# One decoder trunk on one core: adaLN dot products with a loading step of their own, spread over the GLU and the first MLP, and group 6 of that MLP as block products

## The chip, the cores and the metric

The kernel runs on one core of one Trainium2 chip. The metric is the device time of one execution in microseconds (us), the median over several runs; lower is better.

## The reference

The program computes a trunk of two layers on x of 1024 tokens by 1024 features, in float32. Each sub-layer is preceded by an RMS norm that is scaled and shifted by values which depend on one vector c ("adaLN"), and its result is gated by a third such value. Cut to what matters here:

```python
def ada_chunks(c, w, b, n):
    m = jnp.einsum('bd,de->be', jax.nn.silu(c), w) + b
    return jnp.split(m, n, axis=-1)
...
    for i in range(DEPTH):                       # DEPTH = 2
        sh_a, sc_a, g_a, sh_m, sc_m, g_m = ada_chunks(c, ada_w[i], ada_b[i], 6)
        if i < N_A_LAYERS:                       # layer 0: S5 and a GLU
            h = modulate(rms_norm(x, mix_norm_g[i]), sh_a, sc_a)
            y = s5_mixer(h, ...)
            val, gate = jnp.split(jnp.einsum('bsd,de->bse', jax.nn.gelu(y), s5_w_glu[j]), 2, axis=-1)
            mix = val * jax.nn.sigmoid(gate)
        else:                                    # layer 1: attention
            kv_shift, kv_scale = ada_chunks(c, kv_ada_w, kv_ada_b, 2)
            hkv = modulate(rms_norm(x, kv_norm_g), kv_shift, kv_scale)
            ...
        x = x + g_a[:, None, :] * mix
        h = modulate(rms_norm(x, mlp_norm_g[i]), sh_m, sc_m)
        ff = jnp.einsum('bsf,fd->bsd', jnp.square(jax.nn.relu(jnp.einsum('bsd,df->bsf', h, mlp_w1[i]))), mlp_w2[i])
        x = x + g_m[:, None, :] * ff
```

The 112 columns of 128 values that all `ada_chunks` yield together are 112 matrix rows of dot products with silu(c).

## The kernel before

**Stages.** The work runs through S5 (0 to about 235 us of the profile), the GLU (to 411), the first MLP (to about 1130), attention (to about 1850) and the second MLP. Features lie on partitions, tokens in the free dimension in two halves h of 512.

**Matrix products.** TensorE works on fp32r values, so each float32 operand is split into a high and a low part and each product is three matmuls of 128x512 (`mm3`, L251 to L253). A weight unit of 128x1024 is loaded by SyncE's queue into a tile `raw`, cast by ScalarE to its high part `uh` (L217), and VectorE subtracts to get `ul` (`split_unit`, L84). The pool of `raw` tiles has three buffers.

**Dot products.** A dot product (`gemv`, L177) loads 128x1024 of the adaLN weights into a tile of the same pool, and VectorE multiplies it by the row `silr` and sums it into one column of `mod` (or `bias`, for 24 that come from `wT`). After eight of them a small addition ends the chunk, and some chunks also give a column block of `scl`.

**Keep jobs.** GpSimd (POOL) prepares attention's weights meanwhile: `keep` loads 128x512 (L231), scales it (L78; not for `wo`), casts the high part (L236), subtracts (L84) and writes both parts to device memory (`kh`, `kl`, L239). There are 16 jobs for `wo`, 32 for `wkv`, 16 for `wq`; the last 48 need `scl` columns of the chunk M_KSC. Two pairs of tiles `e` take turns.

**GLU.** For output block i of 8 and half h, `glu(i, h)` makes 48 matmuls, ScalarE's sigmoid `g`, VectorE's `g` times the value product, and the gated sum into `xall`. Then follows the norm of the MLP: for each half a small chain on `rw` gives the reciprocal root, and `norm.apply` makes for each k of 8 a tile f (L93, `f<-xall,scl,f`), its high part on ScalarE and its low part `h` (L93, `h<-f,mod,h`), which the next matmuls read. Half 0 is applied around glu(7, 1), half 1 in the first part of the MLP.

**First MLP.** The hidden dimension is cut into 8 groups c of four blocks. Group 0's four up products run for half 0, then for half 1 (the "first part"); after that each group's down products run between the up products of the next group. An up product's result goes through ReLU on ScalarE (`ra`, `rb`), is squared on VectorE and split into `f` tiles. In the second MLP, groups 1 to 7 use `seven`: the 2x2 block products of the down step as seven instead of eight, with POOL making the combined weight blocks.

**Order.** The program is written as engine calls, and a scheduler that works with its own estimates sets each engine's order when the program is built. Calls `pump(n)` in the source take the next jobs (dot products and keep jobs mixed) off a queue and emit them there: nine after each GLU block, three or four at each `mid`, which stand between the steps of the MLP groups.

Of the kernel before, what the change touches and what calls it, by code (L numbers as in the profile page):

```python
# [13 lines left out]
ALU = mybir.AluOpType  # L14
# [42 lines left out]
def kernel(ctx, tc, A, out):  # L57
# [47 lines left out]
    def open_x(i):  # L105
        es = ExitStack()
        pools["x"] = es.enter_context(tile_pool(f"xp{i}", bufs=16 if i else 1))
        pools["raw"] = es.enter_context(tile_pool(f"raw{i}", bufs=3))
        es.callback(pools.pop, "raw")
        turns.clear()  # L110
        return es

    def open_ax(i):
        es = ExitStack()
        pools["ax"] = es.enter_context(tile_pool(f"pax{i}", bufs=4 if "pv" in pools else 6, space=PSUM))
        return es
# [16 lines left out]
    def open_pv():  # L133
        es = ExitStack()
        pools["pv"] = es.enter_context(tile_pool("ppv", bufs=2, space=PSUM))
# [88 lines left out]
    def keep(key, src, c, scale=None):  # L224
# [653 lines left out]
    class Inner:  # L878
# [37 lines left out]
    def mlp(layer, xs, hs, norm, fs, mid=None, done=None, place=None):  # L916
# [124 lines left out]
        def fast(c):  # L1041
            return layer == 1 and c > 0
# [443 lines left out]
    pools["un"] = ctx.enter_context(tile_pool("unp", bufs=3))  # L1486
# [4 lines left out]
    rowp = ada_es.enter_context(tile_pool("rowp", bufs=1))  # L1491
# [295 lines left out]
```

## Time and profile before

| | |
|---|---|
| median of 3 runs | 2519.7 us (2517.2 to 2522.97) |
| profiled execution | 2516.43 us, span 2514.7 us |
| mean granted TensorE clock | 0.974 of 2.4 GHz |
| TensorE busy | 93% of the span |
| VectorE busy | 70% |
| ScalarE busy | 37% |
| GpSimd busy | 36% |

The span goes from the first to the last instruction; the execution's own time is 1.7 us longer. Busy shares are means over stages with different limits.

### The profile page before, as it was taken

The page shows a single profiled execution, that of the slowest core. Times are in us where ns is not written, and L with a number is a line of the kernel's source. Part 1 is how long each engine was busy: PE and PEld are TensorE (multiplying, and loading weights), DVE is VectorE, ACT ScalarE, POOL GpSimd, SP SyncE. Part 2 cuts the span into 40 slices and gives each one's busy share as a digit, 9 for nine tenths or more (in the row PEclk, how much of TensorE's full clock was granted, in tenths as well). Part 3 has the DMA queues.
Part 4 walks back from the last instruction along what each step waited for, and adds up shares of the span by engine and source line. Part 5 has one row for each costly group of instructions (what it writes and reads, how often), then busy time and mean ns, then how long its engine had stood idle before and what let it go on. Part 6 is the DMA issues. An engine that isn't in the chain of part 4 may idle for free.

```text
span 2514.7 us, 33271 instructions
## 1 busy us (share of the span) xinstructions
PE 2350.6 (93%) x12552; PEld 1979.3 (79%) x12552; DVE 1754.3 (70%) x2570; ACT 941.8 (37%) x1710; POOL 909.5 (36%) x965
## 2 busy tenths in 40 slices
PE   3888999989999999999899999998999999999998
PEld 2677788867778888888888888887778888888886
DVE  7997557766776545345687877788583667876787
ACT  5653124211111222133566666676351232223221
POOL 4664460378775000014333323343110322342334
PEclk8899999999999999998999999999999999999999
DMA  4225863667766333123211111126721011111112
GB/s 150 86 79 188 283 221 105 216 241 251 252 239 217 101 117 126 45 89 102 81 58 39 64 68 68 59 100 213 250 78 57 34 51 59 60 42 51 56 54 76
DMA packets 105344, 297.08 MB, mean 118 GB/s; under 512 B 13280, under 2 KB 25568, under 8 KB 105184
## 3 DMA queue, kind: packets, MB, share of 16 engines
q1 hardware_dynamic: 87264, 240.42, 27.9%
q0 software_dynamic: 15360, 50.34, 5.5%
q10 hardware_dynamic: 2560, 4.20, 0.7%
q8 instruction: 99, 1.62, 0.3%
q14 instruction: 61, 0.50, 0.1%
HBM read 241.23 MB, written 49.48 MB: 116 GB/s over the span
## 4 chain that ended last, share of the span: by engine, by line
PE 61%; DVE 17%; DMA 11%; issue 5%; ACT 2%; POOL 1%; SPq 0%; DVEq 0%; POOLq 0%; ACTq 0%
DMA raw<-in_adaT_dram 8%; PE pm L70 8%; PE pm L251 8%; PE pm L252 8%; PE pm L253 8%; PE pa L1001 3%; PE pa L999 3%; PE pa L1000 3%; PE pt L70 3%; DVE sn L1282 3%; DVE raw L177 2%; PE pa L253 2%; PE pa L251 2%; PE pa L252 2%; PE po L70 2%
## 5 line engine op out<-in xcount | busy, mean ns | idle before, releaser
L251 PE MATMUL pm<-h,uh 128*128 128x512 f32 x1192 | 465.6, 393 | 19.3 <-ACT rb L927 15.8
L253 PE MATMUL pm<-h,ul 128*128 128x512 f32 x1192 | 465.5, 391 | 4.7 <-DVE ul L84 4.7
L252 PE MATMUL pm<-h,uh 128*128 128x512 f32 x1192 | 466.3, 391 | 1.6 <-DVE h L93 1.6
L217 ACT CAST uh<-raw 128x1024 fp32r<-128x1024 f32 x130 | 136.7, 1051 | 486.9 <-PE pa L252 154.5
L84 DVE TENSOR_TENSOR ul<-raw,uh 128x1024 fp32r<-128x1024 f32 (+1 forms) x158 | 202.7, 1283 | 126.5 <-ACT uh L217 103.8
L251 PEld LDWEIGHTS pm<-h,uh 128*128 128x128 f32 x1192 | 225.0, 189 | 71.5 <-ACT rb L927 19.3
L177 DVE CUSTOM_DVE_ANT_0 raw<-raw,silr 128x1024 f32<-128x1024 f32 x119 | 162.5, 1369 | 155.4 <-DMA raw<-in_adaT_dram 140.6
L253 PEld LDWEIGHTS pm<-h,ul 128*128 128x128 f32 x1192 | 225.1, 189 | 52.5 <-DVE ul L84 5.6
L252 PEld LDWEIGHTS pm<-h,uh 128*128 128x128 f32 x1192 | 225.3, 189 | 48.6 <-DVE h L93 2.2
L70 PE MATMUL pm<-uh,h 128*128 128x256 f32 x1024 | 238.5, 301 | 3.8 <-DVE rs L1138 3.0
L1282 DVE TENSOR_TENSOR_SCAN sn<-sn 128x768 f32<-128x768 f32 (+7 forms) x128 | 180.6, 1417 | 46.5 <-ACT sn L1277 45.2
L81 POOL TENSOR_TENSOR f<-f,f 128x512 f32<-128x512 f32 x30 | 44.0, 1468 | 397.3 <-ACT f L831 397.2
L70 PEld LDWEIGHTS pm<-uh,h 128*128 128x128 f32 x1024 | 181.7, 199 | 5.0 <-DVE rs L1138 3.4
L81 POOL TENSOR_TENSOR raw<-raw 128x256 f32<-128x256 f32 x28 | 26.0, 929 | 411.4 <-DVE ul L84 411.4
L251 PE MATMUL pa<-f,uh 128*128 128x512 f32 x396 | 154.4, 390 | 1.7 <-DVE xall L93 1.0
L252 PE MATMUL pa<-f,uh 128*128 128x512 f32 x396 | 154.1, 389 | 0.0
L253 PE MATMUL pa<-f,ul 128*128 128x512 f32 x396 | 153.7, 389 | 0.0
L70 PE MATMUL pm<-ul,h 128*128 128x256 f32 x512 | 148.7, 290 | 0.9 <-DMA ul<-kl 0.9
L78 POOL TENSOR_TENSOR sg<-sg,sn 128x512 f32<-128x512 f32 x64 | 93.0, 1453 | 122.5 <-DVE sn L1282 56.3
L70 PE MATMUL pm<-h,uh 128*128 128x512 f32 x402 | 133.7, 414 | 0.0
L93 DVE SCALAR_TENSOR_TENSOR x<-pa,mod,x 128x512 f32<-128x512 f32 x143 | 103.3, 743 | 43.5 <-PE pa L253 29.6
L1277 ACT ACTIVATE sn<-z,rrr 128x512 f32<-128x512 f32 (+1 forms) x192 | 111.6, 581 | 46.9 <-PE z L70 45.4
(380 smaller groups left out, 5497.7 us busy)
## 6 DMA issues: line engine op xcount, KB each, us to landing
raw<-in_w_dram SPq DMA_DIRECT2D x140, 512.0 KB, 3.3
raw<-in_adaT_dram SPq DMA_DIRECT2D x96, 512.0 KB, 3.7
uh<-kh SPq DMA_DIRECT2D x40, 512.0 KB, 4.2
ul<-kl SPq DMA_DIRECT2D x40, 512.0 KB, 4.0
kh<-e POOLq DMA_DIRECT2D x64, 256.0 KB, 2.7
kl<-e POOLq DMA_DIRECT2D x64, 256.0 KB, 3.6
raw<-in_wT_dram SPq DMA_DIRECT2D x24, 512.0 KB, 4.3
raw<-in_wglu_dram SPq DMA_DIRECT2D x20, 512.0 KB, 4.7
```

The lines of the kernel that those rows point to most:

```text
L70: return lambda *a, **k: tc.keep_in_program_order(f(*a, **k))
L78: eng.tensor_tensor(o, a, b, op=ALU.mult)
L84: eng.tensor_tensor(o, a, b, op=ALU.subtract)
L93: V.scalar_tensor_tensor(o, a, s, b, op0=op0, op1=op1)
L177: V.tensor_tensor_reduce(raw, raw, row, 1.0, 0.0, op0=ALU.mult, op1=ALU.add, accum_out=bcol)
L217: ACT.copy(uh, raw)
L251: T.matmul(ps, uh[:, sl], hi, start=first, stop=False)
L252: T.matmul(ps, uh[:, sl], lo, start=False, stop=False)
L253: T.matmul(ps, ul[:, sl], hi, start=False, stop=last)
L999: T.matmul(p, uh[:, sl], hi, start=(i == 0), stop=False)
L1277: ACT.activation(g[:, HN * hb + c0:HN * hb + HN], p[:, c0:], AF.Sigmoid, scale=pj.rr[:, 2, t, a:a + 1])
L1282: V.tensor_tensor_scan(g[:, s0:], g[:, s0:], g[:, s0:], 1.0, op0=ALU.mult, op1=ALU.bypass)
```

## The change

All dot products but one become objects `Gemv` with a pool of their own, "g", of two tiles `gv`; each `pump` runs the next ng of them and then issues the loads of the next two. The pool of `raw` tiles of layer 0 goes from three to two. Seven gate columns, which were computed outright after the first GLU block, join the queue. The chunk M_KSC moves up to the GLU's part of the queue. Dot products are pumped in the GLU two or three per half block, at every `mid`, and at eight new `mid(True)` in the MLP's first part; keep jobs have a list of their own and come one or two per GLU half block and one per `mid`, with one pair of `e` tiles instead of two. `fast` makes group 6 of the first MLP use the seven block products. Several pools drop the option `reuse_waits="tile"` and use the default way to wait for memory that is used again (these lines are left out below).

```diff
-        pools["raw"] = es.enter_context(tile_pool(f"raw{i}", bufs=3))
...
+        pools["raw"] = es.enter_context(tc.tile_pool(name=f"raw{i}", bufs=3 if i else 2))
...
-    def gemv(src, row, bcol):
-        raw = raw_tile()
-        SP.dma_start(raw, src)
-        V.tensor_tensor_reduce(raw, raw, row, 1.0, 0.0, op0=ALU.mult, op1=ALU.add, accum_out=bcol)
+    def product_sum(raw, bcol):
+        V.tensor_tensor_reduce(raw, raw, silr, 1.0, 0.0, op0=ALU.mult, op1=ALU.add, accum_out=bcol)
+
+    class Gemv:
+
+
+        def __init__(self, src, bcol):
+            self.src, self.bcol, self.raw = src, bcol, None
+
+        def load(self):
+            if self.raw is None:
+                self.raw = fs0.pools["g"].tile([P, 1024], F32, tag="gv", name=nm("gv"), bufs=2)
+                SP.dma_start(self.raw, self.src)
+
+        def __call__(self):
+            self.load()
+            product_sum(self.raw, self.bcol)
...
     def ada_chunk(c0, after=None):
-        def one(i):
...
-        return [(lambda i=i: one(i)) for i in range(c0, c0 + 8)] + [fin]
-
-    side = []
-
-    def pump(n):
-        for _ in range(min(n, len(side))):
-            side.pop(0)()
-
-    def queue(jobs, n, others):
-        while jobs or others:
-            side.extend(jobs[:n] + others[:1])
-            del jobs[:n], others[:1]
+        return [Gemv(A["adaT"][i - 16], mod[:, i:i + 1]) for i in range(c0, c0 + 8)] + [fin]
+
+    gems, keep_jobs = [], []
+
+    def pump(ng, nk=0):
+        n = 0
+        while gems and (n < ng or not isinstance(gems[0], Gemv)):
+            job = gems.pop(0)
+            n += isinstance(job, Gemv)
+            job()
+        for job in [j for j in gems if isinstance(j, Gemv)][:2]:
+            job.load()
+        for _ in range(min(nk, len(keep_jobs))):
+            keep_jobs.pop(0)()
...
-        while len(keeps) < 4:
-            keeps.append(fs0.extra((F32, F32R)[len(keeps) % 2]))
-        raw, hi = keeps[0:2] if c == 0 else keeps[2:4]
+        if not keeps:
+            keeps.extend((fs0.extra(F32), fs0.extra(F32R)))
+        raw, hi = keeps
...
         def fast(c):
-            return layer == 1 and c > 0
+            return c > 0 if layer else c == 6
...
             for f in range(4):
                 u = load_unit(w1[f])
                 plain(0, f, h, up(f, u, h))
+                if mid is not None:
+                    mid(True)
                 if h == 0 and f == 0:
...
     def gate(i):
         c = M_GA0 + i
-        gemv(A["adaT"][c - 16], silr, mod[:, c:c + 1])
-        add(mod[:, c:c + 1], mod[:, c:c + 1], adab[:, c:c + 1])
+        if i == 0:
+            raw = raw_tile()
+            SP.dma_start(raw, A["adaT"][c - 16])
+            product_sum(raw, mod[:, c:c + 1])
+            add(mod[:, c:c + 1], mod[:, c:c + 1], adab[:, c:c + 1])
+            return []
+        return [Gemv(A["adaT"][c - 16], mod[:, c:c + 1]),
+                lambda: add(mod[:, c:c + 1], mod[:, c:c + 1], adab[:, c:c + 1])]
...
-    fs.open("a")
-    fs.open("e")
+    for name in "age":
+        fs.open(name)
...
+    with tc.tile_pool(name="gp", bufs=1) as gp:
+        for i in range(1, 8):
+            gems.extend(gate(i))
+        gems.extend(ada_chunk(M_SHM0) + ada_chunk(M_SCM0, lambda: scale_cols(2, M_SCM0)) + ada_chunk(M_GM0)
+                    + ada_chunk(M_KSC, lambda: scale_cols(4, M_KSC)))
+        keep_jobs.extend((lambda i=i, c=c: keep(("o", i), A["wo"][i], c)) for i in range(8) for c in range(2))
...
             ug, uv = first if i == 0 else (load_unit(A["wglu"][8 + i]), load_unit(A["wglu"][i]))
             for h in range(2):
                 glu(i, ug, uv, h)
-                if i == 0:
-                    for c in range(1 + 3 * h, 4 + 4 * h):
-                        gate(c)
-            if i:
-                pump(9)
+                pump(2 + (i == 0), 1 + (i > 2))
...
-    pump(99)
-    side.extend(ada_chunk(M_KSC, lambda: scale_cols(4, M_KSC)) + ada_chunk(M_SCA1, lambda: scale_cols(1, M_SCA1)))
-    queue(ada_chunk(M_KSH) + ada_chunk(M_SHA1) + ada_chunk(M_GA1) + ada_chunk(M_SHM1)
...
+    pump(0, 99)
+    keep_jobs.extend((lambda hp=hp, n=n, c=c: keep(("kv", hp, n), A["wkv"][hp, n], c, scl[:, 32 + 4 * n:36 + 4 * n]))
+                     for hp in range(8) for n in range(2) for c in range(2))
...
     def place(k):
         if k == 0:
-            pump(999)
-            fs.close("b", "e")
+            pump(999, 999)
+            fs.close("b", "e", "g")
...
-    cyc = [0]
-
-    def mid():
-        cyc[0] += 1
-        pump((3, 4)[cyc[0] % 2])
+    gems.extend(ada_chunk(M_SCA1, lambda: scale_cols(1, M_SCA1)))
+    for c0 in (M_KSH, M_SHA1, M_GA1, M_SHM1):
+        gems.extend(ada_chunk(c0))
+    gems.extend(ada_chunk(M_SCM1, lambda: scale_cols(3, M_SCM1)) + ada_chunk(M_GM1)
+                + [lambda: shift_row(M_KSH)] + bias_jobs(0, 16)
+                + [lambda: shift_row(M_SHA1)] + bias_jobs(16, 24) + [kq_gain])
+
+    def mid(first=False):
+        pump(2, 0 if first else 1)
```

On VectorE, in the first part of the MLP, where `norm.apply` makes half 1's tiles (`f` and `h`; `ra` and `ul` belong to the up products), 12 successive rows of before:

```order
L93 SCALAR_TENSOR_TENSOR f_3354<-xall,scl,f_3352 128x512
L93 SCALAR_TENSOR_TENSOR f_3360<-xall,scl,f_3352 128x512
L84 TENSOR_TENSOR f_3551<-ra_3547,f_3550 128x512
L84 TENSOR_TENSOR f_3606<-ra_3602,f_3605 128x512
L93 SCALAR_TENSOR_TENSOR h_3616<-f_3354,mod,h_3615 128x512
L93 SCALAR_TENSOR_TENSOR h_3621<-f_3360,mod,h_3620 128x512
L93 SCALAR_TENSOR_TENSOR f_3354<-xall,scl,f_3352 128x512
L84 TENSOR_TENSOR ul_3772<-raw_3769,uh_3771 128x1024
L93 SCALAR_TENSOR_TENSOR f_3360<-xall,scl,f_3352 128x512
L78 TENSOR_TENSOR ra_3686<-ra_3686 128x512
L93 SCALAR_TENSOR_TENSOR h_3626<-f_3354,mod,h_3625 128x512
L93 SCALAR_TENSOR_TENSOR h_3631<-f_3360,mod,h_3630 128x512
```

and the rows of after at the same step (`gv` rows are the dot products, each with a row that reads its sum):

```order
L93 SCALAR_TENSOR_TENSOR h_3617<-f_3343,mod,h_3616 128x512
L93 SCALAR_TENSOR_TENSOR h_3622<-f_3349,mod,h_3621 128x512
L175 ISA gv_5292,mod<-gv_5292,silr 128x1024
L175 ISA mod 128x1
L84 TENSOR_TENSOR f_3691<-ra_3687,f_3690 128x512
L84 TENSOR_TENSOR ul_3836<-raw_3833,uh_3835 128x1024
L93 SCALAR_TENSOR_TENSOR f_3343<-xall,scl,f_3341 128x512
L78 TENSOR_TENSOR ra_3732<-ra_3732 128x512
L93 SCALAR_TENSOR_TENSOR f_3349<-xall,scl,f_3341 128x512
L175 ISA gv_5294,mod<-gv_5294,silr 128x1024
L175 ISA mod 128x1
L175 ISA gv_5368,mod<-gv_5368,silr 128x1024
```

From the last GLU gate product (the row that reads the last `pm` into `g`) to the last `h` tile of half 1 there are 20 dot products in the order of after, and none in that of before; the applying of half 0 stands wholly behind that gate product in after, and partly ahead of it in before.

On POOL, in the keep jobs of `wkv`, nine rows of before, in which two jobs overlap (`e_2492` with `e_2493`, `e_2494` with `e_2495`):

```order
L78 TENSOR_TENSOR e_2494<-e_2494,scl 128x512
L236 CAST e_2495<-e_2494 128x512
L231 DMA e_2492<-in_wkv_dram 128x512
L84 TENSOR_TENSOR e_2494<-e_2494,e_2495 128x512
L239 DMA kh_5483<-e_2495 128x512
L239 DMA kl_5484<-e_2494 128x512
L78 TENSOR_TENSOR e_2492<-e_2492,scl 128x512
L236 CAST e_2493<-e_2492 128x512
L231 DMA e_2494<-in_wkv_dram 128x512
```

and nine of after, where every job uses the same two tiles:

```order
L78 TENSOR_TENSOR e_2296<-e_2296,scl 128x512
L248 CAST e_2297<-e_2296 128x512
L84 TENSOR_TENSOR e_2296<-e_2296,e_2297 128x512
L251 DMA kh_5296<-e_2297 128x512
L251 DMA kl_5297<-e_2296 128x512
L243 DMA e_2296<-in_wkv_dram 128x512
L78 TENSOR_TENSOR e_2296<-e_2296,scl 128x512
L248 CAST e_2297<-e_2296 128x512
L84 TENSOR_TENSOR e_2296<-e_2296,e_2297 128x512
```

A load now stands behind both writes of the job before it. In after the keep jobs of `wkv` and `wq` run on until the first two block rows (`raw` 128x256) of group 6 stand between the last two of them.

In the GLU, VectorE rows of after between the gate products of blocks (3, 1) and (4, 0):

```order
L78 TENSOR_TENSOR g_2811<-pv_2762,g_2811 128x512
L93 SCALAR_TENSOR_TENSOR xall<-g_2811,mod,xall 128x512
L84 TENSOR_TENSOR ul_2998<-raw_2995,uh_2997 128x1024
L175 ISA gv_3069,mod<-gv_3069,silr 128x1024
L175 ISA mod 128x1
L175 ISA gv_3141,mod<-gv_3141,silr 128x1024
L175 ISA mod 128x1
L175 ISA gv_3143,mod<-gv_3143,silr 128x1024
L175 ISA mod 128x1
L175 ISA gv_3545,mod<-gv_3545,silr 128x1024
L175 ISA mod 128x1
L78 TENSOR_TENSOR g_2897<-pm_2848,g_2897 128x512
```

From the gate product of (2, 1) to that of (7, 1) the order of after holds 43 dot products, four or five for each of ten half blocks. In before it holds seven there, all ahead of that of (4, 0).

## Rows read from the trace of the kernel before

**Rows 1.** The page's first part: busy us, share, instructions
```profile
PE 2350.6 (93%) x12552; PEld 1979.3 (79%) x12552; DVE 1754.3 (70%) x2570; ACT 941.8 (37%) x1710; POOL 909.5 (36%) x965
```

**Rows 2.** Windows: length; PE, PEld, DVE, ACT, POOL busy; clock, DMA share, GB/s
```profile
225.00:292.00 67.00, 63.52 (x281) 52.16 (x278) 36.05 (x53) 14.72 (x23) 26.93 (x30) 0.97 0.85 293
292.00:410.00 118.00, 113.31 (x494) 93.02 (x493) 65.01 (x80) 30.37 (x41) 57.20 (x67) 0.97 0.57 198
410.00:444.00 34.00, 34.00 (x159) 28.09 (x157) 31.62 (x54) 19.70 (x29) 0.00 (x0) 1.00 0.24 79
...
500.00:760.00 260.00, 240.70 (x1033) 194.59 (x1032) 179.26 (x194) 46.24 (x66) 202.38 (x237) 0.98 0.70 248
...
2011.80:2389.00 377.20, 377.20 (x1665) 312.43 (x1665) 276.85 (x375) 107.38 (x160) 120.33 (x105) 1.00 0.16 53
```

**Rows 3.** TensorE's waits, 225 to 1140 us: total, times, longest
```profile
PE pm L251 <- ACT rb L927: 15.8, 7, 6.5
PE pm L253 <- DVE ul L84: 4.7, 2, 3.2
```

**Rows 4.** DVE in order of time near the end of the GLU stage
```profile
404.73 1.41 DVE L93 SCALAR_TENSOR_TENSOR f<-xall,scl,f 128x512 f32<-128x512 f32 x2 [3.13 <-ACT f L857]
...
410.80 0.68 DVE L78 TENSOR_TENSOR g<-pm,g 128x512 f32<-128x512 f32 x1
...
441.60 1.63 DVE L93 SCALAR_TENSOR_TENSOR h<-f,mod,h 128x512 fp32r<-128x512 f32 x2
```

**Rows 5.** DVE by line, 401.6 to 455.9 us, while POOL idles
```profile
L93 DVE SCALAR_TENSOR_TENSOR f<-xall,scl,f 128x512 f32<-128x512 f32 x16 | 11.7, 744 | 3.1 <-ACT f L857 3.1
...
L84 DVE TENSOR_TENSOR ul<-raw,uh 128x1024 fp32r<-128x1024 f32 x9 | 11.0, 1221 | 3.3 <-ACT uh L217 3.3
L78 DVE TENSOR_TENSOR ra<-ra 128x512 f32<-128x512 f32 x7 | 4.8, 684 | 0.0
...
L177 DVE CUSTOM_DVE_ANT_0 raw<-raw,silr 128x1024 f32<-128x1024 f32 x2 | 2.5, 1225 | 1.6 <-DMA raw<-in_adaT_dram 1.6
L93 DVE SCALAR_TENSOR_TENSOR rw<-rw 128x4 f32<-128x4 f32 x6 | 1.0, 162 | 0.2
...
L177 DVE DVE_READ_ACCUMULATOR2_ANT mod<- 128x1 f32 x2 | 0.2, 82 | 0.0
```

**Rows 6.** The same view, 505 to 790 us, with POOL at work
```profile
L177 DVE CUSTOM_DVE_ANT_0 raw<-raw,silr 128x1024 f32<-128x1024 f32 x45 | 66.2, 1471 | 80.2 <-DMA raw<-in_adaT_dram 80.2
L84 DVE TENSOR_TENSOR ul<-raw,uh 128x1024 fp32r<-128x1024 f32 x23 | 37.0, 1610 | 0.0
...
L78 DVE TENSOR_TENSOR ra<-ra 128x512 f32<-128x512 f32 x12 | 14.0, 1170 | 0.0
```

**Rows 7.** The same view, 257 to 340 us, GLU stage
```profile
L93 DVE SCALAR_TENSOR_TENSOR xall<-g,mod,xall 128x512 f32<-128x512 f32 x7 | 6.3, 894 | 0.1
```

**Rows 8.** POOL by line, 500 to 790 us
```profile
L84 POOL TENSOR_TENSOR e<-e,e 128x512 f32<-128x512 f32 x45 | 58.6, 1302 | 1.1
L78 POOL TENSOR_TENSOR e<-e,scl 128x512 f32<-128x512 f32 x43 | 55.2, 1284 | 33.1 <-DMA e<-in_wkv_dram 22.1 <-DMA e<-in_wq_dram 10.5
L236 POOL CAST e<-e 128x512 fp32r<-128x512 f32 x43 | 42.6, 991 | 2.7
```

**Rows 9.** DMA issues, 500 to 790 us: KB each, us to landing
```profile
kl<-e POOLq DMA_DIRECT2D x45, 256.0 KB, 3.6
e<-in_wkv_dram POOLq DMA_DIRECT2D x28, 256.0 KB, 3.4
```

**Rows 10.** DMA issues, 257 to 340 us
```profile
raw<-in_adaT_dram SPq DMA_DIRECT2D x19, 512.0 KB, 3.6
raw<-in_wglu_dram SPq DMA_DIRECT2D x10, 512.0 KB, 5.1
```

**Rows 11.** Windows in which TensorE ran at the lower clock
```profile
532.30:539.10 6.80, 2.88 (x7) 2.31 (x8) 6.12 (x7) 2.06 (x3) 6.63 (x8) 0.50 0.63 226
651.70:655.10 3.40, 3.40 (x10) 2.63 (x9) 1.87 (x2) 2.06 (x3) 3.38 (x5) 0.51 0.51 193
```

More of the change, by code (lines that the diff above doesn't have):

```diff
@@ L106, in open_x @@
         es = ExitStack()
-        pools["x"] = es.enter_context(tile_pool(f"xp{i}", bufs=16 if i else 1))
-        pools["raw"] = es.enter_context(tile_pool(f"raw{i}", bufs=3))
+        pools["x"] = es.enter_context(tc.tile_pool(name=f"xp{i}", bufs=16 if i else 1))
+        pools["raw"] = es.enter_context(tc.tile_pool(name=f"raw{i}", bufs=3 if i else 2))
         es.callback(pools.pop, "raw")
@@ L114, in open_ax @@
         es = ExitStack()
-        pools["ax"] = es.enter_context(tile_pool(f"pax{i}", bufs=4 if "pv" in pools else 6, space=PSUM))
+        pools["ax"] = es.enter_context(tc.tile_pool(name=f"pax{i}", bufs=4 if "pv" in pools else 6, space=PSUM))
         return es
@@ L134, in open_pv @@
         es = ExitStack()
-        pools["pv"] = es.enter_context(tile_pool("ppv", bufs=2, space=PSUM))
+        pools["pv"] = es.enter_context(tc.tile_pool(name="ppv", bufs=2, space=PSUM))
         es.callback(pools.pop, "pv")
@@ L263, in s5 @@
         es = ExitStack()
-        sp = es.enter_context(tile_pool("sp", bufs=1))
-        pp = es.enter_context(tile_pool("s5ps", bufs=2, space=PSUM))
+        sp = es.enter_context(tc.tile_pool(name="sp", bufs=1))
+        pp = es.enter_context(tc.tile_pool(name="s5ps", bufs=2, space=PSUM))
         cst = sp.tile([P, C_N], F32, name="cst")
@@ L885, in open @@
             self.es[name] = ExitStack()
-            self.pools[name] = self.es[name].enter_context(tile_pool("fp" + name))
+            self.pools[name] = self.es[name].enter_context(tc.tile_pool(name="fp" + name, bufs=1))
         def close(self, *names):
@@ L1483, in attention @@
         return oh, ou[-2:]
-    pools["un"] = ctx.enter_context(tile_pool("unp", bufs=3))
+    pools["un"] = ctx.enter_context(tc.tile_pool(name="unp", bufs=3))
     x_es = open_x(0)
@@ L1490 @@
     ada_es = ExitStack()
-    rowp = ada_es.enter_context(tile_pool("rowp", bufs=1))
+    rowp = ada_es.enter_context(tc.tile_pool(name="rowp", bufs=1))
     silr = rowp.tile([P, D], F32, name="silr")
@@ L1522 @@
     fs = fs0 = Inner()
-    fs.open("a")
-    fs.open("e")
+    for name in "age":
+        fs.open(name)
     norm = Norm(norm_tiles(fs), xs, hs, 2, M_SHM0)
-    with tile_pool("gp", bufs=1) as gp:
-        queue(ada_chunk(M_SHM0) + ada_chunk(M_SCM0, lambda: scale_cols(2, M_SCM0)) + ada_chunk(M_GM0), 2,
-              [(lambda i=i, c=c: keep(("o", i), A["wo"][i], c)) for i in range(8) for c in range(2)])
+    with tc.tile_pool(name="gp", bufs=1) as gp:
[4 more added lines that the diff above has]
+        keep_jobs.extend((lambda i=i, c=c: keep(("o", i), A["wo"][i], c)) for i in range(8) for c in range(2))
         def glu(i, ug, uv, h):
@@ L1577, in bias_jobs @@
     def bias_jobs(lo, hi):
[L1578 to L1588 removed]
+        return [Gemv(A["wT"][i], bias[:, i:i + 1]) for i in range(lo, hi)]
+    pump(0, 99)
+    keep_jobs.extend((lambda hp=hp, n=n, c=c: keep(("kv", hp, n), A["wkv"][hp, n], c, scl[:, 32 + 4 * n:36 + 4 * n]))
+                     for hp in range(8) for n in range(2) for c in range(2))
+    keep_jobs.extend((lambda hp=hp, c=c: keep(("q", hp), A["wq"][hp], c, scl[:, 8:16]))
+                     for hp in range(8) for c in range(2))
     brow = cp.tile([P, 2, 128], F32, name="brow")
```

8 lines of the change are left out of this document (removed).

## The prediction

> **What bounds the kernel now.** I read the page's first part, then windows by stage, then TensorE's waits, then single rows of VectorE. TensorE is busy for 2350.6 us of 2514.7 [rows 1], so the kernel is near TensorE's own work, and only the stages where TensorE stands still leave something to gain; equally, a new hold-up on another engine costs time at once. The windows [rows 2] show where it stands still between 225 and 760 us: 3.5 us in the first window and 4.7 us in the second (both GLU), none from 410 to 444 us (the norm's applying and the first up products), and 19.3 us (260.00 less 240.70) from 500 to 760 us, in the first MLP's early groups. The waits [rows 3] name the releasers: 15.8 us end with an `rb` of ScalarE and 4.7 us with a `ul` of VectorE. Behind the `rb` stands VectorE again: its in-order queue has 45 dot products between 505 and 790 us and waits 80.2 us for their loads [rows 6], with the squaring of the next up result behind them. So the first MLP of before is held up by late loads of dot products.
>
> A change in one stage counts here by what TensorE does in it. From 410 to 444 us it works 34.00 of 34.00 us, and VectorE 31.62, while POOL does nothing [rows 2].
>
> **The norm's applying, the largest term.** In the order of after 20 dot products stand among VectorE's rows from the last gate product to the last `h` tile of half 1; before there is none. TensorE can't begin the second half's up products without these tiles, and its order is the same in both kernels, so it has no other work to take in front. Before, this stretch takes 32.4 us, from 410.80 to the end of the last `h` rows, 441.60 + 1.63 [rows 4], and TensorE never waits, for half 0 was partly applied from 404.73 us on. After, these rows are 102: 20 products and 20 rows that read a sum, 33 scalar_tensor_tensor rows of 128x512 (16 f, 16 h, one for `xall`), 5 `ul`, 10 other rows of 128x512, and 14 small ones.
>
> Their sum by the prices that hold while POOL idles [rows 5] is 20 x (1.225 + 0.082) + 33 x 0.744 + 5 x 1.221 + 10 x 0.684 + 14 x 0.162 = 26.1 + 24.6 + 6.1 + 6.8 + 2.3 = 65.9 us. Nothing in this stretch can be faster than that, since the rows stand in one queue. By the prices with POOL at work it is 20 x (1.471 + 0.082) + 33 x 0.894 + 5 x 1.610 + 10 x 1.170 + 2.3 = 31.1 + 29.5 + 8.1 + 11.7 + 2.3 = 82.7 us [rows 6, 7]. POOL is idle there before and isn't after: M_KSC is finished in the GLU, so that the keep jobs of `wkv` begin right behind those of `wo`. With one pair of `e` tiles a job is a load, scale, cast, subtraction and the landing of its writes in series, 3.4 + 1.284 + 0.991 + 1.302 + 3.6 = 10.6 us [rows 8, 9]. Before, a job took 290 / 45 = 6.4 us at 202.38 / 260 = 78% of POOL busy [rows 2, 8], thus 5.0 us of POOL's time; in 10.6 us that is 47%. I take the same share of the step between the two sums, 0.47 / 0.78 = 0.6, which gives 65.9 + 0.6 x 16.8 = 76 us. TensorE stands still for what this exceeds the 32.4 us of before: **+43.6 us**, between +33.5 and +50.3.
>
> The slower prices of VectorE beside a busy POOL are a row of this trace: `ul` takes 1610 ns against 1221, `ra` 1170 against 684 [rows 5, 6]. The Trainium skill, page "SBUF — State Buffer", section "Who interferes with whom" with its diagram's reading in "SBUF: two separate sides", says that an operation of VectorE with two inputs in SBUF and one of GpSimd exclude each other from a shared port pair for the length of a whole instruction. This trace agrees, and the rule speaks against this change, which puts POOL's chain beside the norm. By the rule alone, with POOL computing 3.6 of 10.6 us and half a POOL instruction (0.6 us) as the mean loss of each of the 68 large rows so met, the stretch would be 65.9 + 14 = 80 us (an estimate), and the whole sum 4 us higher.
>
> **The GLU.** From the gate product of (2, 1) to that of (7, 1) there are now 43 dot products, seven before. TensorE's part there is 10 half blocks of 48 matmuls at 377.20 / 1665 = 0.2266 us [rows 2], 109 us, and of 118 us there before 4.7 were waits, and a little went to the lower clock: before the stretch took about 115. The two tiles `gv` turn round in landing plus product: 3.6 + 1.3 = 4.9 us at the least, 5.1 + 1.55 = 6.65 us if they land as late as the GLU's weights do [rows 5, 6, 10]. For 43 products on two tiles that is 105 us (hidden behind the 109 of TensorE) to 143 us. The transfers alone: 43 x 0.52 MB, some 16 weight units of the same size and 10 keep jobs of 0.79 MB are 39 MB; the window at 225 us moved 293 GB/s at a DMA share of 0.85 [rows 2], 345 at a full one, thus 112 us. I take a turn of 5.7 us, the middle, so 122 us: **+7**, ends -6 (TensorE's 109) and +28. A gate product that comes late stops TensorE soon, because its products' accumulators are freed by it.
>
> **The lower clock.** TensorE ran at 0.50 and 0.51 of its clock, the 1.2 GHz level, in two windows after a standstill [rows 11]: 6.8 us with 2.88 busy and 3.4 us fully busy, which cost 1.4 and 1.7 us. Those two go with the standstills that cause them, and the new standstill in the norm brings one or two: **+2** (0 to 3.4).
>
> **What is given back.** In the groups, VectorE has the fewer dot products for it: of the 95 of `adaT` that are left, 12 remain in group 0's down step and none behind it, and the 24 of `wT` stand in groups 3 to 5. In the group 0 stretch that is one product per 4 us of TensorE's time, with both loads ahead. So I take the 19.3 us back, and the 3.1 us of the clock: **-22.4** (at worst -17, if a quarter of the waits stay). Group 6 drops 24 matmuls of 128x512: 24 x 0.2266 = **-5.4**. In the second MLP, where groups 1 to 7 use this form, TensorE works 377.20 of 377.20 us with POOL busy for 120.33 [rows 2], so its combined blocks are hidden; the smaller `raw` pool leaves two units in flight, which the up products' pace (24 matmuls a half, 5.4 us) covers at a landing of 3.6 us for a load of that size [rows 10].
>
> **At nothing.** The pools' other way of waiting shows at the ends of stages, where the next loads wait for the last readers; before, x is read back only when its attention stage has ended anyway. If a stage's first load comes a landing later, it costs 3 to 5 us (within the range). The keep chain: 48 jobs of 10.6 us from about 420 us end at about 930, and group 6's down step begins past 1000 us; the last jobs stand ahead of its blocks in POOL's queue. That cover of some 70 us is gone if a job takes over 12 us.
>
> **The sum** is against the profiled execution's 2516.4 us (its span 2514.7 and 1.7 around it): 2516.4 + 43.6 + 7 + 2 - 22.4 - 5.4 = 2541.2. That execution is 3.3 us under the median of the three runs, so I predict **2543 us**, 23 us slower. Its ends: 33.5 - 6 + 0 - 22.4 - 5.4 = -0.3, and 50.3 + 28 + 3.4 - 17 - 5.4 = +59; both at once is unlikely. A difference under 0.2%, 5 us, can't be told from none in this measurement.
>
> **The rivals.**
> - The dot products among the norm's rows are hidden (faster). If TensorE had other work during them, the 43.6 us would fall away and the time be 2541.2 - 43.6 = 2498 us. It decides from the point where less than 14 us of the 43.6 are exposed. For it: VectorE waited 3.1 us for ScalarE at 404.73 [rows 4], so there is some slack. Against it: VectorE had 2.4 us idle in 34 [rows 2], and 26 us of products don't go into that. Chance 0.11.
> - The time hardly moves: the applying is at its low end and the GLU hidden behind TensorE, 2516 to 2522 us. For it: the GLU's low price needs only loads at their 3.6 us, which was measured at a DMA share like that of the new stretch. Chance 0.11.
> - POOL's chain holds up VectorE through the whole norm: all prices of [rows 6, 7], 82.7 us, 6.7 more than forecast. That is 2548 and, with the median's 3.3, 2551 us. For it: these jobs are of the same make as those behind [rows 8]; against: only half of POOL's time is taken. Chance 0.15. The rule of the Trainium skill's page "SBUF — State Buffer" named above would be what does it.
> - The GLU is bound by its loads: 43 x 3.3 = 143 us, +28 instead of +7: 2564 us. For it the 112 us of pure transfer, against it the 3.6 us landings in a stretch with 10 weight loads and 19 products [rows 10]. Chance 0.09.
> - The keep chain is late for group 6: at 13 us a job 48 jobs end at 1044 us, 25 to 40 us too late; TensorE would wait 20 us or more: 2563 us. Against it the 70 us of cover. Chance 0.05.
>
> **How the numbers follow.** The forecast, +43.6 and what goes with it, has the chance 0.49 and reaches by itself from 2530 to 2553. The range for 8 in 10 takes in the unmoved time and the lesser half of the two late cases: 2513 to 2563 us. Slower by over 0.2% are the forecast and three rivals, 0.49 + 0.15 + 0.09 + 0.05 = 0.78; same 0.11, faster 0.11.
>
> **What would show it.** In the changed kernel's trace, TensorE should stand still for some 45 us between the last GLU matmul and group 0's down step, ended by `h` rows of VectorE, with the chain of waits leading through L93 and the dot products there; VectorE should be nearly full in that stretch and POOL busy. From there to 760 us the waits on `rb` should be gone, with no lower clock. The GLU's end should come within 10 us of 411. The down step of group 6 should be about 5 us shorter, with no wait on `uh` or `ul` from POOL. The prediction is wrong if TensorE stays full through the norm, or if standstills move into groups 1 to 7, which I take to be full.

## The result, and the profile of the changed kernel

The changed kernel takes 2538.41 us (median of 4 runs, 2535.75 to 2542.64), the kernel before 2518.45 us on the same chip (4 runs): a ratio of 1.008, with a 95% interval of 1.0058 to 1.0103. It is about 20 us slower, where 2543 us had been forecast. Its profiled span is 2536.7 us, 22.0 longer than that of before. The later experiments ran on three chips, on which the kernel before takes 2524 to 2526 us; each is compared by its ratio to the kernel before on its own chip.

The page's first part hardly differs from [rows 1]:

```profile
PE 2356.4 (93%) x12528; PEld 1981.6 (78%) x12528; DVE 1773.1 (70%) x2612; ACT 947.5 (37%) x1720; POOL 955.6 (38%) x989
```

The windows by stage do. Columns as in [rows 2]:

```profile
292.00:410.00 118.00, 102.28 (x423) 82.28 (x422) 84.34 (x117) 21.81 (x30) 42.73 (x44) 0.94 0.80 273
410.00:444.00 34.00, 24.19 (x91) 18.50 (x89) 30.93 (x58) 7.89 (x11) 11.38 (x13) 0.80 0.83 276
444.00:500.00 56.00, 37.07 (x128) 25.70 (x129) 51.90 (x78) 18.84 (x27) 22.77 (x27) 0.88 0.74 258
500.00:760.00 260.00, 260.00 (x1148) 215.25 (x1147) 137.84 (x157) 53.77 (x74) 127.08 (x137) 1.00 0.44 154
```

TensorE, full from 410 to 444 us before, works 24.19 of 34 us and then 37.07 of 56, and at a granted clock of 0.80 and 0.88. From 500 us on it is full, 260.00 of 260, where it stood still for 19.3 us before. The waits of TensorE from 225 to 1160 us (total, times, longest) say what holds it up; both names of [rows 3] are gone or changed:

```profile
PE pm L264 <- DVE h L93: 15.5, 9, 3.8
PE pm L263 <- ACT h L886: 9.1, 4, 6.1
PE pm L265 <- DVE ul L84: 7.7, 3, 3.9
PE pm L263 <- ACT g L1564: 5.3, 1, 5.3
```

These are the `h` tiles of the norm's applying, from VectorE and ScalarE, and in the GLU `ul` and `g`. Two rows of VectorE bound the norm's stretch, as [rows 4] did:

```profile
425.92 0.69 DVE L78 TENSOR_TENSOR g<-pm,g 128x512 f32<-128x512 f32 x1
...
496.55 0.74 DVE L93 SCALAR_TENSOR_TENSOR h<-f,mod,h 128x512 fp32r<-128x512 f32 x1
```

From 425.92 to 497.29 us it takes 71.4 us (32.4 before), and it begins 15.1 us later. In the chain of waits there is nothing but VectorE's queue and loads for it, here for ten of its microseconds (start, length, what):

```profile
444.52 1.67 DVE h L93
446.20 1.14 DVE gv L175
447.42 0.66 DVE f L93
448.08 0.66 DVE h L93
448.74 1.14 DVE gv L175
449.92 4.01 DMA gv<-in_adaT_dram
453.95 2.21 DVE gv L175
```

Dot products (`gv`) stand between the `f` and `h` rows that TensorE wants, and one of them waits for its load. At the last `h` tile of half 1 the changed kernel is 54.1 us behind; at the first result of group 6's down step it is 25.0 behind (1049.87 against 1024.82), at that of group 7 20.8, at the end 22.0.

### The profile page after: what moved, and what is told of

Read it like the earlier page. It is cut to its first block, busy times and chain, and to the rows that moved or that the text cites. A ratio compares the mean times of both kernels' runs of the same rounds, so it can differ in the third digit from the quotient of the medians.

```text
span 2536.7 us, 33352 instructions
## 1 busy us (share of the span) xinstructions
PE 2356.4 (93%) x12528; PEld 1981.6 (78%) x12528; DVE 1773.1 (70%) x2612; ACT 947.5 (37%) x1720; POOL 955.6 (38%) x989
## 4 chain that ended last, share of the span: by engine, by line
PE 69%; DVE 14%; DMA 8%; issue 3%; ACT 3%; POOL 1%; SPq 0%; DVEq 0%; ACTq 0%; POOLq 0%
PE pm L263 9%; PE pm L264 9%; PE pm L265 9%; PE pm L70 8%; DMA gv<-in_adaT_dram 5%; PE pa L1013 4%; PE pa L1011 4%; PE pa L1012 4%; PE pa L265 3%; PE pa L263 3%; PE pa L264 3%; PE pt L70 3%; DVE sn L1296 3%; PE z L70 2%; PE po L70 2%
## 5 line engine op out<-in xcount | busy, mean ns | idle before, releaser
L175 DVE CUSTOM_DVE_ANT_0 gv<-gv,silr 128x1024 f32<-128x1024 f32 x119 | 158.8, 1339 | 100.3 <-DMA gv<-in_adaT_dram 83.3
L263 PE MATMUL pa<-f,uh 128*128 128x512 f32 x364 | 141.7, 389 | 0.0
L265 PE MATMUL pa<-f,ul 128*128 128x512 f32 x364 | 141.6, 389 | 0.0
L264 PE MATMUL pa<-f,uh 128*128 128x512 f32 x364 | 141.6, 389 | 0.0
L84 DVE TENSOR_TENSOR wt<-pt,wt 128x512 fp32r<-128x512 f32 (+1 forms) x160 | 100.8, 630 | 36.4 <-ACT wt L1324 30.2
```

Of the source, the lines that this page charges most:

```text
L84: eng.tensor_tensor(o, a, b, op=ALU.subtract)
L175: V.tensor_tensor_reduce(raw, raw, silr, 1.0, 0.0, op0=ALU.mult, op1=ALU.add, accum_out=bcol)
L263: T.matmul(ps, uh[:, sl], hi, start=first, stop=False)
L264: T.matmul(ps, uh[:, sl], lo, start=False, stop=False)
L265: T.matmul(ps, ul[:, sl], hi, start=False, stop=last)
```

## The experiments

Kernels are edits of the changed kernel unless said otherwise. Dot products in an order are counted on VectorE "in the GLU" from gate product (2, 1) to (7, 1) and "in the norm" from there to the last `h` tile of half 1: 43 and 20 in the changed kernel. The program without the eight `mid(True)` calls has the same 43 and 20 in VectorE's order and wasn't run: the scheduler moves the products forward by itself, with or without these calls.

**Group 6 alone, both ways.** One kernel undoes it in the changed kernel, the other does it alone in the kernel before (the same line the other way round):

```diff
-            return c > 0 if layer else c == 6
+            return layer == 1 and c > 0
```

> The changed kernel with group 6 of the first MLP as plain products again. If the seven block products are worth their 24 matmuls and nothing else (24 x 0.2266 = 5.4 us), the time is 2538.4 + 5.4 = 2544 us and TensorE's first 500 us are as in the changed kernel. Rival: POOL's blocks cost as much as they save; then it stays at 2538 us.

> The kernel before with group 6 of the first MLP as seven block products and nothing else of the change. If this part adds up with the rest, 2518.5 - 5.4 = 2513 us, ratio 0.998, and nothing else moves. Rival: group 6 of this kernel waits for its blocks, because its weight tiles are shared with the dot products; then no gain or a loss of some us.

Undone: 2547.12 us, ratio 1.0081 (1.0068 to 1.0094). Alone: 2524.47 us, ratio 0.9983 (0.9968 to 0.9998), thus 4.3 us less. The ratio of the undone kernel can't be told from the changed kernel's 1.008, which is from another chip; on its own chip it takes 7.6 us more than the next experiment's kernel (2539.56 us), which has the changed kernel's order on VectorE. From the first down result of group 6 to that of group 7 the profile has 71.9 us in the changed kernel and 76.2 undone (4.3 us), and attention's first scan comes at 1237.6 and 1245.1 (7.5 us). So the part is worth 4 to 8 us, which agrees with the 5.4 us of its 24 matmuls.

**The pools' waits.** All pools get `reuse_waits="tile"` back:

```diff
-    pools["un"] = ctx.enter_context(tc.tile_pool(name="unp", bufs=3))
+    pools["un"] = ctx.enter_context(tile_pool("unp", bufs=3))
```

> The changed kernel with the pools' option reuse_waits="tile" put back everywhere. The order on VectorE is the same. My theory: pools' waits are worth 0 to 3 us at the ends of stages, so 2535 to 2538 us. Rival: the default waits cost 5 us or more at the start of the GLU (where the first dot product's load waits for all readers of S5's memory) and at the end of attention: 2533 us or less.

2539.56 us, ratio 1.0056 (1.0042 to 1.0069), an interval that overlaps the changed kernel's; its span is 2537.0 against 2536.7 us, and the last `h` tile comes at 496.2 against 497.3. No effect that could be told.

**Dot products held back behind the norm.** A tiny write of `silr`, on which all later products depend, waits for the last `h` tile:

```diff
-    pump(0, 99)
+    pump(99, 99)
...
-                if mid is not None:
-                    mid(True)
...
                     norm.apply(1, 0, 8)
+                    if hold is not None:
+                        hold()
...
+    def hold():
+        stt(silr[:, 0:1], hs[7][1][1][:, 0:1].bitcast(F32), 0.0, silr[:, 0:1], ALU.mult, ALU.add)
```

> The changed kernel, but dot products of M_SCA1 and later need a column of silr that is written again (with its own value) after the last h tile of half 1, so that none of them can stand in the norm or the GLU; those up to M_KSC are emitted ahead of the first MLP. In its order the norm's stretch holds none and the stretch from gate product (2, 1) to (7, 1) 23 instead of 43; 80 come later. My theory: the norm takes 33 to 36 us again instead of 71.4, the GLU ends 10 to 20 us earlier (near 411), and the loads ahead still spare half or more of the 26 us that group 0 to 3 lost before: 2485 to 2500 us. Rival: the dot products cost their loads wherever they stand, so that the groups lose the 26 us again: 2505 to 2515 us. A second rival, that the GLU and the norm were long for another reason than the dot products: still near 2538 us.

2526.43 us, ratio 1.0003 (0.9989 to 1.0017). The first half of the theory held: the GLU's last gate product stands at 409.8 us and the norm takes 38.5 us, so that the last `h` tile comes 49 us earlier than in the changed kernel. But 36 us of it are lost again by the end, outside the 2485 to 2500 us expected. TensorE stands still for 25.8 us behind the norm (1.0 in the changed kernel) and runs at the lower clock for some 24 us there, most of it within or just behind these waits; some 6 us of the 36 I can't place. TensorE's waits behind the norm (448 to 1135 us) show where:

```profile
PE pa L1011 <- ACT e L945: 15.9, 1, 15.9
PE pm L263 <- ACT ra L939: 5.3, 2, 4.3
PE pm L263 <- ACT rb L939: 3.1, 1, 3.1
```

8.4 us of waits for `ra` and `rb` go in groups 0 and 1 and at their start, where 56 of the 80 products now stand. The larger wait is of another kind. On VectorE, in group 6:

```profile
1017.51 0.69 DVE L81 TENSOR_TENSOR rb<-pv,rb 128x512 f32<-128x512 f32 x1
1039.64 0.69 DVE L84 TENSOR_TENSOR e<-rb,e 128x512 fp32r<-128x512 f32 x1 [21.44 <-DMA kl<-e]
```

A tile `e` for the block products' operands waits 21.44 us for a keep job's write. In the changed kernel the last such write and the first `e` row of group 6 stand as follows (POOL's row, the median landing of these writes in us behind it, VectorE's row):

```profile
1037.76 0.54 POOL L251 DMA_DIRECT2D kl<-e  x1
```

```profile
kl<-e POOLq DMA_DIRECT2D x54, 256.0 KB, 2.9
```

```profile
1042.69 0.69 DVE L84 TENSOR_TENSOR e<-rb,e 128x512 fp32r<-128x512 f32 x1
```

The write lands at about 1040.7 us and the tile is wanted at 1042.69: the chain of keep jobs is just in time. Whatever makes the first stages faster meets it.

**The turn of the `gv` tiles.** Four tiles, loaded four ahead; to make room, group 6 is plain and layer 0 has two `e` tiles:

```diff
-                self.raw = fs0.pools["g"].tile([P, 1024], F32, tag="gv", name=nm("gv"), bufs=2)
+                self.raw = fs0.pools["g"].tile([P, 1024], F32, tag="gv", name=nm("gv"), bufs=4)
...
-        for job in [j for j in gems if isinstance(j, Gemv)][:2]:
+        for job in [j for j in gems if isinstance(j, Gemv)][:4]:
...
-            return self.pools["e"].tile([P, HN], dt, tag="e", name=nm("e"), bufs=8)
+            return self.pools["e"].tile([P, HN], dt, tag="e", name=nm("e"), bufs=2 if self is fs0 else 8)
```

> The changed kernel without the seven block products in group 6 (that frees e tiles) and with four gv tiles and loads four ahead. The scheduler moves still more dot products forward: 50 instead of 43 between gate products (2, 1) and (7, 1), 26 instead of 20 in the norm. My theory: the GLU is slow by the turn of two tiles (129.8 us for 43, 3.0 each); with four tiles the 50 take 110 to 120 us, and VectorE's waits for gv loads, 54 us between 243 and 426 us, fall under 20. The norm takes 80 to 85 us. Rival: the GLU is bound by the transfers themselves; then the 50 products take 145 us or more, and the waits stay.

> The kernel of e5_four_gv timed in rounds. From its one profile: 27 us shorter up to the end of the GLU, the norm as long as in the changed kernel, and 5.4 us more in group 6: ratio 0.996 to 0.999 to the kernel before. Rival: its one time was a chance of that run, and it lies at 1.000 to 1.004.

A single time was 2518.76 us; the median of 12 is 2522.55 us, ratio 0.9992 (0.9982 to 1.0002), just above the 0.996 to 0.999 expected and not to be told from the kernel before. In the two profiles the GLU part took 109.2 and 111.5 us for 50 products, as long as the 109 us estimated for TensorE alone, where the changed kernel took 129.8 for 43. VectorE's waits for these loads from 243 to 426 us (total, times, longest), first in the changed kernel, then with four tiles:

```profile
DVE gv L175 <- DMA gv<-in_adaT_dram: 54.3, 34, 7.4
```

```profile
DVE gv L175 <- DMA gv<-in_adaT_dram: 13.9, 12, 7.2
```

So the GLU was bound by the turn of two tiles and not by the transfers. But the transfers come near with four: the DMA share in the GLU part is then 0.95 (0.81 in the changed kernel), and VectorE is busy for 105.31 of its 109.16 us. The norm took 73.2 and 73.7 us with 26 products, below the 80 to 85 expected.

**POOL idle in the norm.** Keep jobs behind the eleventh need a tile that POOL writes from the last `h` tile:

```diff
-                pump(2 + (i == 0), 1 + (i > 2))
+                pump(2 + (i == 0), int(i + h > 0))
...
-    pump(0, 99)
...
+    def hold():
+        G.tensor_copy(keeps[1][:, 0:1], hs[7][1][1][:, 0:1])
```

> The changed kernel, but only 11 keep jobs of wo are emitted in the GLU, and all later ones need a tile that POOL writes from the last h tile of half 1: POOL has next to nothing in the norm's stretch. Read here is that stretch, from gate product (7, 1) to the last h tile; it has 22 dot products and 107 rows instead of 20 and 102. The keep chain must come late for group 6, so the whole time says nothing about it (2560 to 2610 us). My theory of prices: at the prices of an idle POOL 65.9 us and 2.6 for the two more products, 66 to 69 us, and h tiles at 0.745 us instead of 0.890. Rival: VectorE's slower prices come of DMA traffic and not of POOL; then the stretch stays at 71 to 74 us.

**Two pairs of `e` tiles**, as before the change:

```diff
-        if not keeps:
-            keeps.extend((fs0.extra(F32), fs0.extra(F32R)))
-        raw, hi = keeps
+        while len(keeps) < 4:
+            keeps.append(fs0.extra((F32, F32R)[len(keeps) % 2]))
+        raw, hi = keeps[0:2] if c == 0 else keeps[2:4]
```

> The changed kernel with two pairs of e tiles for the keep jobs, as before the change. Its order has 39 dot products from gate product (2, 1) to (7, 1) and 18 in the norm (43 and 20 in the changed kernel). The keep chain, whose last write landed 2 us ahead of group 6's first need in the changed kernel, ends 100 us or more earlier. My theory: that chain is just not late, so this gives only what the four and two products fewer give, ratio 1.003 to 1.008 to the kernel before. Rival: POOL's faster jobs cost VectorE and the loads more than the products spare; then 1.008 or more.

The norm's stretch with POOL idle (one run, 2570.09 us in all, with the late keep chain that it makes): its window, and VectorE's rows in it.

```profile
429.85:496.13 66.28, 45.25 (x153) 33.12 (x154) 60.88 (x110) 21.14 (x30) 0.00 (x0) 0.77 0.71 226
```

```profile
L175 DVE CUSTOM_DVE_ANT_0 gv<-gv,silr 128x1024 f32<-128x1024 f32 x24 | 29.3, 1222 | 6.1 <-DMA gv<-in_adaT_dram 5.9
...
L93 DVE SCALAR_TENSOR_TENSOR h<-f,mod,h 128x512 fp32r<-128x512 f32 x16 | 11.5, 748 | 0.0
```

In the changed kernel, 426 to 498 us, with POOL busy for 27.99 of 71.43 us of it:

```profile
L175 DVE CUSTOM_DVE_ANT_0 gv<-gv,silr 128x1024 f32<-128x1024 f32 x21 | 27.8, 1326 | 4.4 <-DMA gv<-in_adaT_dram 4.2
L93 DVE SCALAR_TENSOR_TENSOR h<-f,mod,h 128x512 fp32r<-128x512 f32 x16 | 14.0, 890 | 0.0
L93 DVE SCALAR_TENSOR_TENSOR f<-xall,scl,f 128x512 f32<-128x512 f32 x16 | 12.1, 763 | 0.0
L84 DVE TENSOR_TENSOR ul<-raw,uh 128x1024 fp32r<-128x1024 f32 x5 | 6.1, 1218 | 0.0
L78 DVE TENSOR_TENSOR ra<-ra 128x512 f32<-128x512 f32 x4 | 3.8, 952 | 0.0
```

And with two pairs, where POOL is busy for 55.70 of 81.88 us:

```profile
431.83:513.71 81.88, 49.59 (x155) 34.37 (x154) 78.54 (x102) 21.33 (x31) 55.70 (x60) 0.73 0.75 253
```

```profile
L175 DVE CUSTOM_DVE_ANT_0 gv<-gv,silr 128x1024 f32<-128x1024 f32 x20 | 30.1, 1503 | 2.0 <-DMA gv<-in_adaT_dram 2.0
L93 DVE SCALAR_TENSOR_TENSOR h<-f,mod,h 128x512 fp32r<-128x512 f32 x16 | 17.7, 1129 | 0.0
```

The same stretch with four `gv` tiles (e5_four_gv), where POOL is busy for 22.71 us:

```profile
398.85:472.06 73.21, 46.78 (x155) 33.84 (x154) 71.97 (x119) 21.43 (x31) 22.71 (x26) 0.72 0.85 300
```

```profile
L175 DVE CUSTOM_DVE_ANT_0 gv<-gv,silr 128x1024 f32<-128x1024 f32 x27 | 33.9, 1258 | 0.7 <-DMA gv<-in_adaT_dram 0.7
L93 DVE SCALAR_TENSOR_TENSOR h<-f,mod,h 128x512 fp32r<-128x512 f32 x16 | 12.6, 808 | 0.3
```

At POOL's shares of 0, 31, 39 and 68% a dot product takes 1222, 1258, 1326 and 1503 ns and an `h` row 748, 808, 890 and 1129, at DMA shares of 0.71, 0.85, 0.75 and 0.75. The prices follow POOL and not the transfers: the highest DMA share goes with the second lowest price. So it is POOL that slows VectorE here, and 66.3 us with 22 products lies in the 66 to 69 us expected from the prices of [rows 5]. The kernel with two pairs takes 2565.97 us, ratio 1.0153 (1.0137 to 1.017): my theory of it failed and its rival held. Its 18 products in the norm cost more than the 20 of the changed kernel, its GLU ends 5.9 us later, and from the last `h` tile to the end it takes 11 us more. The single pair, which slows the keep jobs, is thus a gain of this change of some 0.7%, by the two ratios (1.0153 and 1.008, from two chips; their intervals allow 0.3 to 1.1%).

**Held back, with two pairs.**

> The kernel with held-back dot products (the run e3_held) and two pairs of e tiles. In e3_held TensorE waited once for 15.9 us in group 6 for e tiles whose keep writes landed at 1039.5 us, and ran at the lower clock behind it. My theory: with a faster keep chain this goes, 16 us of wait and some 6 us of clock, and 7 us of waits in group 0 stay: ratio 0.990 to 0.993 to the kernel before. Rival: faster keep jobs slow the loads of the dot products in groups 0 to 3, where the kernel before lost 26 us; then 0.996 to 1.001.

2549.29 us, ratio 1.0089 (1.0071 to 1.0106): the rival by its time, and by more than it said. Of the 24.8 us by which its span exceeds that of e3_held, 6.3 are lost up to the GLU's end and 7.5 in the norm (46.0 us instead of 38.5). The wait in group 6 is gone, but the waits behind the norm grow from 25.8 us, of which group 6's was 15.9, to 32.9. Windows behind the norm and VectorE's dot products there, first of this kernel, then of e3_held:

```profile
462.00:675.00 213.00, 180.10 (x754) 144.50 (x752) 171.23 (x203) 35.50 (x49) 138.94 (x156) 0.95 0.82 274
```

```profile
L175 DVE CUSTOM_DVE_ANT_0 gv<-gv,silr 128x1024 f32<-128x1024 f32 x56 | 90.4, 1619 | 37.9 <-DMA gv<-in_adaT_dram 37.7
```

```profile
448.00:660.00 212.00, 202.05 (x870) 164.39 (x869) 156.52 (x217) 44.37 (x62) 88.26 (x96) 0.98 0.74 248
```

```profile
L175 DVE CUSTOM_DVE_ANT_0 gv<-gv,silr 128x1024 f32<-128x1024 f32 x56 | 73.3, 1312 | 36.0 <-DMA gv<-in_adaT_dram 35.7
```

A product rises from 1312 to 1619 ns with POOL busy for 65% of the window instead of 42%; VectorE's waits for the loads, which the rival named, stay as they were (37.7 and 35.7 us).

**Held back, with four `gv` tiles.** The edits of e3_held and e5_four_gv together:

> Both findings together: dot products held back behind the last h tile (as in e3_held) and four gv tiles with loads four ahead (as in e5_four_gv, with group 6 as plain products, since the e tiles are given up for them). Its order has 20 dot products from gate product (2, 1) to (7, 1), none in the norm, 80 later. My theory: the GLU ends near 399 us as in e5_four_gv, the norm takes 36 to 39 us as in e3_held, and the rest takes what it took in the changed kernel and 5.4 us for group 6: 399 + 38 + 2036 + 5 + 2 = 2480 us, and up to 15 us for waits in group 0 and 1: ratio 0.982 to 0.990. Rival: 80 products behind the norm cost the groups 20 us or more in spite of four tiles: 0.992 or more.

2482.51 us, ratio 0.9836 (0.9818 to 0.9853): as expected, and some 42 us below the kernel before on its chip (2524.29 us). Its windows, in the columns of [rows 2], and the one of the changed kernel's four waits shown above that is left from 225 to 1140 us:

```profile
292.00:410.00 118.00, 117.11 (x528) 96.80 (x526) 79.59 (x116) 33.19 (x45) 51.67 (x57) 1.00 0.65 229
410.00:444.00 34.00, 30.22 (x135) 24.28 (x135) 33.59 (x48) 17.80 (x26) 15.97 (x18) 1.00 0.57 197
444.00:500.00 56.00, 56.00 (x249) 46.35 (x248) 55.46 (x84) 11.50 (x15) 18.57 (x18) 1.00 0.96 337
500.00:760.00 260.00, 260.00 (x1148) 215.25 (x1147) 150.53 (x180) 52.46 (x72) 121.66 (x132) 1.00 0.50 175
```

```profile
PE pm L264 <- DVE h L93: 2.4, 2, 1.5
```

The GLU's last gate product stands at 397.3 us, the last `h` tile at 434.6, and from there to the end it takes what the changed kernel takes and 4.4 us more, about what the plain group 6 costs.

**Dot products in the pool of `raw` tiles again**, three of them, with the loads two ahead kept:

```diff
-                self.raw = fs0.pools["g"].tile([P, 1024], F32, tag="gv", name=nm("gv"), bufs=2)
+                self.raw = raw_tile()
...
-        pools["raw"] = es.enter_context(tc.tile_pool(name=f"raw{i}", bufs=3 if i else 2))
+        pools["raw"] = es.enter_context(tc.tile_pool(name=f"raw{i}", bufs=3))
```

> The changed kernel, but the dot products take their tiles from the pool of raw tiles (three, shared with the weights, as before the change), still loaded two ahead. Its order has 14 dot products from gate product (2, 1) to (7, 1) and 10 in the norm (43 and 20 in the changed kernel): the shared pool ties them to the weights' order. My theory: it is the pool of their own that lets the products run forward. The norm then takes 32.4 us and 10 x 1.4 and something for POOL, 48 to 54 us, the GLU ends at 410 to 418 us, and the groups wait again for 15 to 25 us: ratio 1.000 to 1.008. Rival: the loads ahead are what matters, with the groups' waits gone also here: below 1.000.

2535.13 us, ratio 1.0059 (1.0034 to 1.0083). The GLU ends at 410.5 us and the norm takes 55.7 with its 10 products, and the groups wait again for 19.0 us, now for weights that are cast late (total, times, longest, 225 to 1140 us):

```profile
PE pm L263 <- ACT uh L229: 14.0, 2, 7.6
```

Loads two ahead in a shared pool of three don't free the groups; with the pool of their own the groups are free and the products run ahead into the GLU and the norm. The shared pool has three tiles in all, where the changed kernel has two and two, so what sharing does and what the fourth tile does isn't told apart.

## Why the prediction was right, by its steps

The span grew by 22.0 us: 15.1 by the GLU's end, 39.0 in the norm, -29.1 in groups 0 to 5, -4.2 in group 6 and 1.2 behind it. The forecast had +7, +43.6, -22.4 and -5.4, and +2 for the clock, which is +24.8. So the mechanisms were right and the terms were not: the GLU was 8 us too small, the norm 5 too large and what is given back 7 too small, and that the total lies within 3 us is in part luck. The 2543 us don't follow from the sum, either: 2541.2 and 3.3 are 2544.5.

- **The norm's applying** was forecast at 76 us between 65.9 and 82.7, +43.6; it took 71.4, +39.0. The mechanism is shown: without products in it the stretch takes 38.5 us, with 22 of them and no POOL 66.3. The step from the low to the high price was a little too large: POOL was busy for 39% of the stretch and not 47%, and with jobs of `wo`, which don't scale, as these loads show:

```profile
L243 POOL DMA_DIRECT2D e<-in_wo_dram x4 | 2.2, 541 | 13.9 <-DMA kl<-e 13.9
L243 POOL DMA_DIRECT2D e<-in_wkv_dram x2 | 1.1, 542 | 5.4 <-DMA kl<-e 5.4
```

- **The rule on the shared port** of the Trainium skill ("SBUF — State Buffer", "Who interferes with whom"), that an operation of VectorE with two inputs in SBUF and one of GpSimd that reads SBUF exclude each other, is borne out in direction by the `h` rows and dot products at the four shares of POOL above. The 80 us worked out from it alone are too much for this stretch (71.4); with two pairs of `e` tiles the stretch did reach 81.9. That POOL's chain holds VectorE at full price through the norm, a rival with the same end, was wrong for the changed kernel and right for that one.
- **The GLU** was forecast at +7 (-6 to +28) and ended 15.1 us late, outside the 10 us named as a sign: the term was under-sized. The turn of the two tiles was the right mechanism (four tiles end it), but I took 5.7 us for it where 129.8 / 43 products show 6.0, so the stretch took 7.8 us more than the 122. The 115 us that I took for it in the kernel before were wrong too. Gate product (2, 1) of before and of after:

```profile
308.21 0.68 DVE L78 TENSOR_TENSOR g<-pv,g 128x512 f32<-128x512 f32 x1
```

```profile
296.08 0.68 DVE L78 TENSOR_TENSOR g<-pv,g 128x512 f32<-128x512 f32 x1
```

  From 308.21 to 410.80 us the stretch of before is 102.6 us, 12.4 less than I took, and after reaches its start 12.1 us earlier, which I hadn't counted; that these two cancel is luck. Of the 12.1 us, 4.2 are there at the first gate product (243.35 against 247.58). Before, TensorE waits 3.5 us at S5's end for a copy that stands on ScalarE behind a cast of late GLU weights, and that gate product stands on VectorE behind dot products; after has neither. The rival of 28 us was too far. The bound by transfers did not hold here: with four tiles the GLU takes TensorE's time.
- **The lower clock** was forecast at +2. TensorE ran at it for 41 us between the first gate product and the last `h` tile, against 6.8 before; the term was under-sized. 17 us of the 41 lie in the GLU, where, with half of the time of its matmuls lost, it cost some 5 us more than before (an estimate), a part of the 15.1. In the norm TensorE waits for VectorE anyway, so I take its cost there as small, which no run shows. It also stood still there for less than the 45 us named as a sign, 25.6 (71.43 less 45.88 busy), since its matmuls were longer.
- **Given back**: -22.4 in groups 0 to 5 was forecast, and 54.1 - 25.0 = 29.1 us came. TensorE's standstill there fell from 20.5 us (the last `h` tile to 1130 us) to 1.0, and the two windows at the lower clock are gone, whose matmuls lost 3.1 us [rows 11]: 22.6 us, the two things forecast. TensorE also has 12 matmuls fewer in the stretch (2448 and 2460), some 3 us; the last 4 I can't place. Group 6 gave 25.0 - 20.8 = 4.2 us against 5.4.
- **At nothing**: the pools' waits cost nothing that could be told, as said. The cover of 70 us for the keep chain was wrong: I let the jobs of `wkv` start at 420 us, but those of `wo` run on to 483, so the chain ends 2 us ahead of its need. It didn't change the time here, and it decided e3_held. I also gave the single pair of `e` tiles no gain of its own.
- **The rivals**: that the 20 products are hidden in the norm is refuted by the held-back kernels. That nothing moves needed the GLU hidden behind TensorE, which took four tiles.

## What to carry to other kernels

Work that is given buffers of its own loses the order that shared buffers had forced on it; look at where a scheduler then puts it, and above all at what it puts ahead of the rows that the bounding engine waits for. Here the same dot products cost 39 us in front of a norm and next to nothing behind it, given enough tiles for their loads. A chain on a side engine that is "hidden" may be so by two microseconds, and making it faster may cost more than its lateness, if its work slows the engine on the path, as POOL's did VectorE's here.

## What the runs showed of the hardware that I had not expected

VectorE's price beside POOL rises with POOL's busy share, and more steeply at the high end (an `h` row 748, 808, 890 and 1129 ns at 0, 31, 39 and 68%); slower keep jobs on one pair of tiles were worth about 0.7% of this kernel. Not all rows pay it. Those that add a matmul's result to `xall` read one of their two tiles from PSUM, the memory that matmuls write. They kept their price where a dot product went from 1312 to 1619 ns, here first in e3_held behind the norm (POOL 42%), then in the same kernel with two pairs (65%):

```profile
L93 DVE SCALAR_TENSOR_TENSOR xall<-pa,mod,xall 128x512 f32<-128x512 f32 x21 | 15.4, 744 | 0.0
```

```profile
L93 DVE SCALAR_TENSOR_TENSOR xall<-pa,mod,xall 128x512 f32<-128x512 f32 x21 | 15.4, 740 | 0.0
```

Loads of 0.5 MB on two tiles gave a product only every 3.0 us, while four tiles gave one every 2.2 us with the same queue, although a load then landed later (a median of 5.6 and 5.7 us in the two profiles instead of 4.4): the tiles and not the transfers set the pace.
